# Two halves of a modulation as VectorE's partial sums in the first feed-forward, in place of TensorE's units at the norm changes

## The chip, the cores and the metric

The kernel runs on one core of a Trainium2 chip. Its engines work side by side, each through its own queue in program order, and meet through semaphores: TensorE (PE in the profile; its loads of the stationary operand are PEld), VectorE (DVE), ScalarE (ACT), GpSimd (POOL) and SyncE (SP), which here issues the loads of all weights. The metric is the device time of one launch in microseconds, as the median of several runs.

## The reference, cut to what matters

One step of a diffusion backbone with one layer on 640 tokens of 1024 channels: 128 context tokens and 512 latent ones. Both groups pass the same weights, but each is modulated by a vector of its own. The modulations are one matrix product of a vector with 9216 columns, nine pieces of 1024:

```python
def trunk_layer(x, cond, ...):
    mod = jax.nn.silu(cond) @ w_mod + b_mod
    sh1, sc1, g1, shm, scm, gm, sh2, sc2, g2 = jnp.split(mod, N_MOD, axis=-1)
    h = modulate(rmsnorm(x, norm_g[0]), sh1, sc1)
    x = x + 0.5 * g1[:, None, :] * swiglu(h, ffn1_w1, ffn1_w2)
    h = modulate(rmsnorm(x, norm_g[1]), shm, scm)
    y, C, n, m = mixer(h, ...)
    x = x + gm[:, None, :] * y
    h = modulate(rmsnorm(x, norm_g[2]), sh2, sc2)
    x = x + 0.5 * g2[:, None, :] * swiglu(h, ffn2_w1, ffn2_w2)
```

`swiglu` splits `h @ w1` in two, multiplies `silu(a)` with `b` and applies w2, with 2816 channels inside. Everything is float32. So gm is needed only where the mixer's output joins x, and g2 only where the second feed-forward's output does; shm and scm are needed at the norm before the mixer, sh2 and sc2 at the norm before the second feed-forward.

## The kernel before

The activations lie transposed in SBUF, channels on the partitions. The 640 tokens are two halves of 320 columns (h = 0 is the left half, h = 1 the right). A float32 product is three matmuls on rounded operands (`three`, L245 to L247): each operand is split into a high part, a cast on ACT (L75), and a low part, the difference on VectorE (L79), and high by high, high by low and low by high are summed in PSUM.

**Elements.** The program is a list of elements that `run` goes through in order. Each names its weight loads (raws of 512 KB or less, which go through a ring of five `wr` slots, issued by SP in the order of the elements), the splits of its weights (made four operations ahead of their use) and a function that emits its work. An element can have a `fill`, small steps spread over its products.

- A **pair** (`pair_el`) makes two column blocks of a first product by a scheme of seven half-size products instead of eight. VectorE forms four sums of weights for it (L218). The order is A11, S1, S2, A12, S3, S4, A22, twelve matmuls each. Behind S3, L294 on VectorE adds a saved product to the accumulator that A22 then goes on summing. Behind S4, L297 adds another. The fill's steps are spread over the seven products: four steps land behind the second, fourth, sixth and seventh.
- A **w2 element** (`plain_el`) makes one block of the second product for both halves, and its results are added to the residual x by VectorE (L937), three operations.
- `halves_el` makes the last blocks before a norm change half by half, so that the left half's norm can start while TensorE makes the right half's blocks.
- `head_el` is the first element behind a norm change: three blocks on the left half, then on the right half. Its chain is the norm: the sum of squares (summed at L801, over the partitions by TensorE at L819), the root and reciprocal, the diagonal matrices (L829) and their spread over the partitions on TensorE (L836), scaling (L844), modulation (L852, L854) and the splits into H11, H21 for the left and T4 ("HT4"), H22 for the right half.

The first feed-forward runs through 22 blocks in groups of 6, 6, 6 and 4: pairs, then eight w2 elements for each group (the last group has two and a `halves_el`). Two norm changes follow in the kernel: first feed-forward to mixer, at some 455 to 500 us of the span, and mixer to second feed-forward, at some 1190 to 1230 us.

**Modulations** are made in three ways.

- `mod_mid(ch, half)`: four loads of a quarter, each followed by four matmuls of the vector with 256 columns on four 32-column groups of TensorE (`mod_half`, L574; a float32 matmul leaves two records). `head_el` takes two of the loads before its products and two between the left and the right half. Then come a copy out of PSUM (L581, one on VectorE, one on ACT), four transposes (L586) and a sum and a bias on VectorE (L591, L593), some later. GM's lower half is made so in the mixer's head, and G2's in the second feed-forward's head.
- `mod_dve(ch, halves, wide, joint)`: four loads of 128 x 1024, each with four VectorE operations of 128x512: the first of a sum multiplies (L694), the others multiply and add (L696) into two accumulators, one for each group of tokens. When a half is summed, three steps follow: TensorE sums the partitions with ones on its four column groups and ACT copies (`red`, L705 and L708), two transposes (`turn`, L713), the bias on VectorE (`fin`, L721). With `joint` the three steps of two halves are put together: one `red` step with eight matmuls (16 records), one `turn`, one `fin`.
- `mod_own`: for the first feed-forward's own gate.

`with_units(main, units, spare)` puts the units (a load and its four VectorE operations) into the elements of `main`: the load comes behind the element's own raws, the operations into its fill, and of the three later steps one goes into each following element. With n elements less the spare ones and m units, unit e goes to element floor(e n / m). In the first feed-forward `main` has 42 elements with 2 spare: w2 elements 0 to 7, pairs 8 to 13, w2 14 to 21, pairs 22 to 27, w2 28 to 35, pairs 36 to 39, w2 40 and 41. The accumulators are four tiles of the pool `ma`.

Of the kernel before, what the change touches and what calls it, by code (L numbers as in the profile page):

```python
# [44 lines left out]
def mixer_step(ctx: ExitStack, tc: tile.TileContext, x_prompt, x_sample, state_C, state_n, state_m,  # L45
# [290 lines left out]
    def head_el(blocks, chain, work, mid=(), extra=None):  # L336


        pre, nb = len(mid) // 2, len(blocks)
        order = [None] * pre + [0, 1, 2] + [None] * (len(mid) - pre) + list(range(3, nb))  # L340
        points = 4 * nb - 6
        at_ = {t: i for i, t in enumerate(order) if t is not None}

        def emit():
            flush()
            n = {"i": 0}

            def take(u, i):
                u["emit"](raw(el["base"] + i))
                rdone.add(el["base"] + i)  # L350
                load_more()

            def some(*_):
                n["i"] += 1
                if n["i"] == 3 and soon:
                    soon.pop(0)()
                while len(work) > 0 and n["i"] * total >= points * (total - len(work) + 1):
                    work.pop(0)()

            total = len(work)  # L360
            ev = lambda t: lambda h_, ps: blocks[t][1](h_, ps)
            hold()
            for i in range(pre):
                take(mid[i], i)
            w = [[op()] for t in range(3)]
            ps = [big() for t in range(3)]
            for k in range(KT):
                if k == 4:
                    for t in range(3):
                        w[t].append(op())  # L370
                for t in range(3):
                    three(ps[t][:, :HT], *w[t][k // 4], k % 4, plain_acts(k, 0), k == 0, k == KT - 1)
                if k == 1:
                    chain[0]()
                    for f in N.pop("rest"):
                        f()
                if k == 3:
                    chain[1]()
            for t in range(3):
                ev(t)(0, ps[t][:, :HT])  # L380
            chain[2]()
            for i in range(pre, len(mid)):
                take(mid[i], 3 + i)
            chain[3]()
            for t in range(3):
                unit(w[t], KT, plain_acts, 1, ev(t), {3: some, 7: some})
                release(2)
            if extra:
                extra()
            for t in range(3, nb):  # L390
                w = [op(), op()]
                unit(w, KT, plain_acts, 0, ev(t), {3: some, 7: some})
                unit(w, KT, plain_acts, 1, ev(t), {3: some, 7: some})
            while work:
                work.pop(0)()
            for f in chain[4:]:
                f()
        loads = [b[0] for b in blocks]
        loads = [u["raws"][0] for u in mid[:pre]] + loads[:3] + [u["raws"][0] for u in mid[pre:]] + loads[3:]
        oa = [dict(tile_ops(KT, at_[t])[i], raws=[at_[t]]) for i in range(2) for t in range(3)]  # L400
        ob = [dict(o, raws=[at_[t]]) for t in range(3, nb) for o in tile_ops(KT, at_[t])]
        el = dict(element(loads, oa + ob, emit), calm=True)
        return el

    def blocks_of(p):
        return [(p[i], lambda h, ps, i=i: p[2](i, h, ps)) for i in range(2)]
# [269 lines left out]
    def mod_dve(ch, halves, wide, joint=False):  # L676


        units, posts = [], []
        for half in halves:  # L680
            hold_ = {}
            for kq in range(4):
                fns = []
                for i in range(2):
                    for k in range(2):
                        def fn(w, i=i, k=k, kq=kq, hold_=hold_):
                            if kq == 0 and k == 0:
                                hold_[i] = wide()
                            s = cm[:, 2 * kq + k, i:i + 1]
                            for j, acc in enumerate(hold_[i]):  # L690
                                n = 512 // len(hold_[i])
                                w_ = w[:, 512 * k + j * n:512 * k + j * n + n]
                                if kq == 0 and k == 0:
                                    V.tensor_scalar(acc, w_, s, None, op0=OP.mult)  # L694
                                else:
                                    V.scalar_tensor_tensor(acc, w_, s, acc, op0=OP.mult, op1=OP.add)  # L696
                        fns.append(fn)

                def red(hold_=hold_):

                    p = aux()
                    n = 512 // len(hold_[0])
                    for q in range(4):
                        i, a = q // 2, 256 * (q % 2)
                        PE.matmul(p[32 * q:32 * q + 32, :256], ones[:, :32], hold_[i][a // n][:, a % n:a % n + 256],  # L705
                                  start=True, stop=True, skip_group_check=True, tile_position=(0, 32 * q))
                    hold_["r"] = t3()
                    A.copy(hold_["r"][:, :256], p[:, :256])  # L708

                def turn(hold_=hold_):  # L710
                    p = hold_["p"] = aux()
                    for j in range(2):
                        PE.transpose(p[:, j * P:j * P + P], hold_["r"][:, j * P:j * P + P], ident)  # L713

                def fin(ch=ch, half=half, hold_=hold_):
                    b0 = ch * KT + 4 * half
                    o = modT[:, ch, 4 * half:4 * half + 4, :].rearrange("p (c j) i -> p i c j", c=2)
                    src = hold_["p"][:, :256].rearrange("p (j i c r) -> p i c j r", j=2, i=2, c=2)[:, :, :, :, 0]
                    b = bmT[:, b0:b0 + 4].rearrange("p (c j) -> p c j", c=2)
                    for i in range(2):  # L720
                        V.tensor_add(o[:, i], src[:, i], b)  # L721
                if kq == 3:
                    posts.append((red, turn, fin))
                more = []
                if kq == 3 and (not joint or half == halves[-1]):
                    more = [lambda fs=fs: [f() for f in fs] for fs in zip(*posts)]
                    posts = []
                units.append((mod_load(ch, half, kq), fns, more))
        return units

    def with_units(main, units, spare=0):

        out = []
        n, m = len(main) - spare, len(units)
        e = 0
        post = []
        for i, el in enumerate(main):
            el = dict(el, raws=list(el["raws"]), fill=list(el.get("fill", ())))
            now, post = post[:1], post[1:]
            while e < m and e * n < (i + 1) * m:  # L740
                load, fns, more = units[e]
                at_ = len(el["raws"])
                el["raws"].append(load)
                for j, fn in enumerate(fns):
                    def go(fn=fn, at_=at_, el=el, last=(j == len(fns) - 1)):
                        fn(raw(el["base"] + at_))
                        if last:
                            rdone.add(el["base"] + at_)
                            load_more()
                    el["fill"].append(step(go))  # L750
                post += [step(f) for f in more]
                e += 1
            el["fill"] += now
            out.append(el)
        assert e == m
        return out + [step(lambda: lazy.extend(p["emit"] for p in post))]
# [534 lines left out]
    main = []  # L1291
    for i in range(3):
        main += els[i][1] + els[i + 1][0]
    w2s = els[3][1]
    prog += with_units(main + w2s[:-1], mod_dve(SHM, (0, 1), ma_wide, True) + mod_dve(SCM, (0, 1), ma_wide, True) +
                   mod_dve(SH2, (0,), ma_wide), 2)
    prog += [step(gain(1, SCM)), step(lambda: PO["ma_x"].close()), w2s[-1]]


# [450 lines left out]

    h0 = head_q(0)
    chain, work = right_chain(1, SHM)
    prog.append(head_el(blocks_of(h0[0]) + blocks_of(h0[1]), chain, work, mod_mid(GM, 0), gate_rows))
    def tanh_first():
        A.activation(tp.tile([P, 3], F32, name="rstd", bufs=2)[:, 0:1], eps, AF.Tanh)

# [230 lines left out]
            YQ.append(y_out)  # L1987

    PO["y"] = y_queue
    head, els = ffn(ffn2_w1, ffn2_w2, G2, y_after, lambda bl: head_el(bl, *right_chain(2, SH2), mod_mid(G2, 0)))  # L1990
    prog += [head] + els[0][0] + [step(half_gate(G2))]
    for i in range(3):
        prog += els[i][1] + els[i + 1][0]
# [30 lines left out]
```

## Time and profile before

| | |
|---|---|
| median of 3 runs | 1662.88 us (1662.47 to 1663.27) |
| span of the profiled execution | 1659.7 us (the page gives no time of its own beside it) |
| granted TensorE clock, mean | 0.999 |
| TensorE busy | 1642.4 us |
| VectorE busy | 1257.6 us |
| ACT busy | 791.5 us |

A line of the timeline reads: start and length in us, engine, line of the kernel, operation, output <- inputs, shape, count, and in brackets how long the engine had been idle before it and who ended the wait. Two matmuls of a stream overlap in the records: 0.31 us is the length of one, but the next one starts about 0.15 us behind it. So what an insertion costs TensorE is read from the starts around it. A line of the page's groups gives line, engine, operation, operands, count | busy us, mean ns of one | idle before it. A line of the chain gives start, us, engine, output and line.

### The profile page before, as it was taken

To read this page: it belongs to the slowest core of one execution; us is meant where nothing else is said; L and a number is where in the kernel's file an instruction comes from. 1 tells how busy PE (TensorE), PEld (TensorE's weight loads), DVE (VectorE), ACT (ScalarE), POOL (GpSimd) and SP (SyncE) were. 2 spreads that over 40 slices of the span, in tenths; PEclk is the share of its full clock that TensorE was granted. 3 is DMA by queue.
4 is the path that set the end of the run, shared out by engine and by line. 5 is a ranking of instruction groups with operands and counts; after the bars stand their busy time and mean duration, and the time that the engine had idled before them with its cause. 6 is when DMAs were issued, how large, how long until landed. Compare 5 with 4: busy or idle time off the path is not lost.

```text
span 1659.7 us, 29315 instructions
## 1 busy us (share of the span) xinstructions
PE 1642.4 (99%) x11201; PEld 1601.4 (96%) x11201; DVE 1257.6 (76%) x2681; ACT 791.5 (48%) x1723; POOL 170.7 (10%) x258
## 2 busy tenths in 40 slices
PE   8999999999999999999999999999999999999998
PEld 5999999999999999999999999999999999999997
DVE  6867877877778878778897898789587467476576
ACT  5642542533566656555561455532375245254253
POOL 2010000000031322111121221011100000000002
PEclk9999999999999999999999999999999999999999
DMA  9454333343352434342367323366241322232222
GB/s 321 115 165 127 111 111 111 102 136 101 108 178 80 113 88 111 75 109 67 96 208 239 106 79 92 101 196 207 90 127 55 99 77 79 74 93 87 77 77 64
DMA packets 273036, 193.08 MB, mean 116 GB/s; under 512 B 7923, under 2 KB 253050, under 8 KB 272896
## 3 DMA queue, kind: packets, MB, share of 16 engines
q1 hardware_dynamic: 263280, 158.36, 32.5%
q0 software_dynamic: 9584, 32.85, 6.8%
q8 instruction: 88, 1.44, 0.4%
q14 instruction: 52, 0.43, 0.1%
q10 hardware_dynamic: 32, 0.01, 0.0%
HBM read 175.87 MB, written 15.31 MB: 115 GB/s over the span
## 4 chain that ended last, share of the span: by engine, by line
PE 91%; DVE 3%; ACT 3%; DMA 2%; issue 1%; SPq 1%; POOL 0%; ACTq 0%; DVEq 0%; POOLq 0%
PE ps L245 28%; PE ps L246 28%; PE ps L247 28%; PE ax L1583 2%; PE ax L1614 2%; DMA wr<-in_ffn_w_dram 1%; PE ax L1586 1%; PE ax L1560 1%; ACT Uh L852 1%; DVE wl L79 0%; ACT wh L75 0%; SPq L552 0%; DVE x L937 0%; DMA wl<-in_x_sample_dram 0%; DVE Uh L844 0%
## 5 line engine op out<-in xcount | busy, mean ns | idle before, releaser
L79 DVE TENSOR_TENSOR wl<-wr,wh 128x512 fp32r<-128x512 f32 (+1 forms) x406 | 265.3, 667 | 79.8 <-ACT wh L75 76.5
L75 ACT CAST wh<-wr 128x512 fp32r<-128x512 f32 (+1 forms) x408 | 237.4, 593 | 158.7 <-PE ps L246 146.1
L79 DVE TENSOR_TENSOR wl<-ws,wh 128x512 fp32r<-128x512 f32 x288 | 203.1, 705 | 44.5 <-ACT wh L75 43.8
L75 ACT CAST wh<-ws 128x512 fp32r<-128x512 f32 x288 | 175.7, 619 | 101.2 <-DVE ws L218 60.0
L245 PE MATMUL ps<-Uh,wh 128*128 128x320 f32 x704 | 218.8, 311 | 0.0
L246 PE MATMUL ps<-Ul,wh 128*128 128x320 f32 x704 | 217.2, 309 | 0.0
L247 PE MATMUL ps<-Uh,wl 128*128 128x320 f32 x704 | 217.2, 308 | 0.0
L937 DVE SCALAR_TENSOR_TENSOR x<-ps,modT,x 128x128 f32<-128x128 f32 (+2 forms) x216 | 82.6, 432 | 114.0 <-PE ps L247 114.0
L245 PEld LDWEIGHTS ps<-Uh,wh 128*128 128x128 f32 x704 | 132.1, 188 | 1.2 <-issue 0.8
L246 PEld LDWEIGHTS ps<-Ul,wh 128*128 128x128 f32 x704 | 132.1, 188 | 0.2 <-DVE Ul L79 0.2
L247 PEld LDWEIGHTS ps<-Uh,wl 128*128 128x128 f32 x704 | 132.1, 188 | 0.0
L245 PE MATMUL ps<-H11h,wh 128*128 128x320 f32 x380 | 120.0, 316 | 0.5 <-ACT H11h L75 0.5
L245 PE MATMUL ps<-HT4h,wh 128*128 128x320 f32 x380 | 119.8, 315 | 0.0
L245 PE MATMUL ps<-H21h,wh 128*128 128x320 f32 x380 | 118.9, 313 | 0.0
L246 PE MATMUL ps<-H11l,wh 128*128 128x320 f32 x380 | 117.7, 310 | 0.3
L246 PE MATMUL ps<-HT4l,wh 128*128 128x320 f32 x380 | 117.5, 309 | 0.1
L247 PE MATMUL ps<-H21h,wl 128*128 128x320 f32 x380 | 117.5, 309 | 0.0
L247 PE MATMUL ps<-HT4h,wl 128*128 128x320 f32 x380 | 117.4, 309 | 0.0
L247 PE MATMUL ps<-H11h,wl 128*128 128x320 f32 x380 | 117.4, 309 | 0.0
L246 PE MATMUL ps<-H21l,wh 128*128 128x320 f32 x380 | 117.2, 308 | 0.0
L245 PE MATMUL ps<-H22h,wh 128*128 128x320 f32 x348 | 108.9, 313 | 0.0
L246 PE MATMUL ps<-H22l,wh 128*128 128x320 f32 x348 | 107.7, 309 | 0.4
(440 smaller groups left out, 4475.6 us busy)
## 6 DMA issues: line engine op xcount, KB each, us to landing
wr<-in_ffn_w_dram SPq DMA_DIRECT2D x86, 512.0 KB, 3.8
wr<-in_w_in_dram SPq DMA_DIRECT2D x72, 512.0 KB, 3.7
wr<-in_w_mod_dram SPq DMA_DIRECT2D x51, 512.0 KB, 3.8
wr<-in_ffn_w_dram SPq DMA_DIRECT2D x48, 384.0 KB, 3.4
early<-in_w_mod_dram SPq DMA_DIRECT2D x13, 512.0 KB, 8.4
wr<-in_ffn_w_dram SPq DMA_DIRECT2D x20, 256.0 KB, 3.2
mg<-in_w_mod_dram POOLq DMA_DIRECT2D x8, 512.0 KB, 5.5
wr<-in_w_ml_out_dram SPq DMA_DIRECT2D x8, 512.0 KB, 4.6
```

The source lines that it names most:

```text
L75: A.copy(hi, raw)
L79: V.tensor_sub(lo, raw, f32(hi))
L245: PE.matmul(ps, hi[:, ws], ah, start=start, stop=False, skip_group_check=True)
L246: PE.matmul(ps, hi[:, ws], al, start=False, stop=False, skip_group_check=True)
L247: PE.matmul(ps, lo[:, ws], ah, start=False, stop=stop, skip_group_check=True)
L852: A.activation(t[:, a:b], t[:, a:b], AF.Identity, scale=sc_, bias=bi_)
L937: V.scalar_tensor_tensor(X[m][:, o + a:o + b], ps[:, a:b], modT[:, g, m, cd:cd + 1], X[m][:, o + a:o + b], op0=OP.mult, op1=OP.add)
L1560: PE.matmul(p[:, :P], S["k", dt][:, sl], S["q", dt][:, sl], start=(dt == 0), stop=(dt == 1))
L1583: PE.matmul(p2[:, :DH + 1], S["q", dt][:, sl], S["C"][d][:, dt, :], start=(dt == 0), stop=(dt == 1))
L1586: PE.matmul(p1[:, :DH + 1], S["p", ch][:, d, :], PO["vt"][:, ch, :], start=True, stop=True)
L1614: PE.matmul(p[:, :DH + 1], kw[:, dt * P:(dt + 1) * P], PO["vt"][:, ch, :], start=True, stop=True)
```

## The change

Two lists change. The first feed-forward's units become seven halves in place of five: the lower halves of GM and G2 join SHM, SCM and SH2's lower half, and the three later steps of SHM and SCM are no longer put together. At the heads of the mixer and of the second feed-forward `mod_mid` is taken out.

```diff
-    prog += with_units(main + w2s[:-1], mod_dve(SHM, (0, 1), ma_wide, True) + mod_dve(SCM, (0, 1), ma_wide, True) +
-                   mod_dve(SH2, (0,), ma_wide), 2)
+    prog += with_units(main + w2s[:-1], mod_dve(SHM, (0, 1), ma_wide) + mod_dve(SCM, (0, 1), ma_wide) +
+                   mod_dve(GM, (0,), ma_wide) + mod_dve(SH2, (0,), ma_wide) + mod_dve(G2, (0,), ma_wide), 2)
...
-    prog.append(head_el(blocks_of(h0[0]) + blocks_of(h0[1]), chain, work, mod_mid(GM, 0), gate_rows))
+    prog.append(head_el(blocks_of(h0[0]) + blocks_of(h0[1]), chain, work, (), gate_rows))
...
-    head, els = ffn(ffn2_w1, ffn2_w2, G2, y_after, lambda bl: head_el(bl, *right_chain(2, SH2), mod_mid(G2, 0)))
+    head, els = ffn(ffn2_w1, ffn2_w2, G2, y_after, lambda bl: head_el(bl, *right_chain(2, SH2)))
```

So m goes from 20 to 28 in the first feed-forward. The same weights are loaded, by as many loads of the same size: eight of them move from the heads to the first feed-forward. The upper halves of GM and G2, and G2's factor of one half, stay where they were.

## The prediction

> **What bounds the kernel now.** I read the page first, then busy time by windows, then TensorE's own order of time around the two norm changes, and last VectorE's order inside the first feed-forward, where the change puts its work.
>
> ```profile
> span 1659.7 us, 29315 instructions
> ...
> PE 1642.4 (99%) x11201; PEld 1601.4 (96%) x11201; DVE 1257.6 (76%) x2681; ACT 791.5 (48%) x1723; POOL 170.7 (10%) x258
> ...
> PE 91%; DVE 3%; ACT 3%; DMA 2%; issue 1%; SPq 1%; POOL 0%; ACTq 0%; DVEq 0%; POOLq 0%
> ```
>
> TensorE is busy 99% of the span, and 91% of the chain that ended last is TensorE. So an edit is priced by the time it takes or frees in TensorE's stream, except where TensorE stands waiting for another engine. The next rows (length, then busy time and count of PE, PEld, DVE, ACT, POOL, then granted clock and DMA) show both kinds of stage.
>
> ```profile
> 197.06:209.38 12.32, 12.32 (x86) 12.32 (x85) 10.68 (x20) 6.63 (x14) 0.00 (x0) 1.00 0.46 129
> 450.00:500.00 50.00, 49.15 (x349) 46.17 (x348) 37.99 (x93) 31.81 (x70) 13.24 (x18) 1.00 0.56 172
> ```
>
> The first window is one period of a w1 pair in the first feed-forward: TensorE is full for all 12.32 us, VectorE is busy 10.68 us of it. The second holds the change from the first feed-forward to the mixer: TensorE is short by 0.85 us there, so something else ends last.
>
> **The change part by part.** First the prices. One STT (the accumulating operation of a partial sum) and the matmuls that go:
>
> ```profile
> L696 DVE SCALAR_TENSOR_TENSOR ma<-wr,cm,ma 128x512 f32<-128x512 f32 x70 | 51.6, 747 | 0.9
> ...
> L574 PE MATMUL ax<-wr,cm 128*32 128x256 f32 x64 | 4.3, 385 | 0.0
> ```
>
> A half of a modulation is four loads of 512 KB and 16 VectorE operations; at 0.747 us each that is at most 12.0 us (the two that open the sums are tensor_scalar and no dearer, I take them at the same price). Two halves more (GM's and G2's lower ones) put 23.9 us on VectorE, and eight loads more on SP's queue, between the elements of the first feed-forward. The 64 matmuls of L574 are what goes: 32 at each norm change, in two blocks of 16 records each. What a block costs TensorE is read where nothing waits, at the second norm change:
>
> ```profile
> 1207.59 0.31 PE L247 MATMUL ps<-HT4h,wl 128*128 128x320 f32 x1
> 1207.83 1.07 PE L574 MATMUL ax<-wr,cm 128*32 128x256 f32 x16
> ...
> 1209.08 0.31 PE L246 MATMUL ps<-H11l,wh 128*128 128x320 f32 x1
> ```
>
> From the last matmul before to the second one behind it 1.49 us pass, where two steps of the stream would be 0.29 (0.146 us each: the twelve from 207.41 to 209.16, in the last rows of this part, take 1.75): **1.20 us** a block, 4.80 for the four. The reductions of a partial sum over the partitions (L705) are read alike, for two halves at once (16 records) and for one (8):
>
> ```profile
> 245.95 0.31 PE L247 MATMUL ps<-Uh,wl 128*128 128x320 f32 x1
> 246.19 1.07 PE L705 MATMUL ax<-ma,ones 128*32 128x256 f32 x16
> ...
> 247.44 0.30 PE L246 MATMUL ps<-Ul,wh 128*128 128x320 f32 x1
> ...
> 446.46 0.31 PE L247 MATMUL ps<-HT4h,wl 128*128 128x320 f32 x1
> 446.70 0.64 PE L705 MATMUL ax<-ma,ones 128*32 128x256 f32 x8
> ...
> 447.52 0.31 PE L246 MATMUL ps<-Ul,wh 128*128 128x320 f32 x1
> ```
>
> 1.49 less 0.29 is 1.20 us for a joint block; 1.06 less 0.29 is **0.77 us** for a single one. Two single ones cost 0.34 more than a joint one. The chain prices the transposes behind them:
>
> ```profile
> 252.73 0.44 PE ax L713 x4
> ...
> 451.05 0.22 PE ax L713 x2
> ```
>
> 0.44 us for four and 0.22 for two, so splitting these costs nothing. mod_mid ends in four such transposes as well (0.44).
>
> A rule bears on this: the Trainium skill, "TensorEngine Tiling (Array Packing)", section "Tiling Modes", says that going from one tiling mode of the array to another drains TensorE. It speaks against the change, which replaces two joint reductions by four: without such a cost a block of 8 would be half of one of 16, 0.60 us, the added TensorE work 2 x (0.60 + 0.22) = 1.64 instead of the 2.66 us below, and the sum 1.0 lower. The rows above have that cost in them, so the trace agrees, and they are used.
>
> So in the **first feed-forward** TensorE gets 2 x 0.34 for the joint reductions of SHM and SCM that are split, and 2 x (0.77 + 0.22) for the new halves: **+2.66 us**. Nothing there hides it, as TensorE never waits. Behind the norm changes the transposes of mod_mid go: 2 x 0.44 = **-0.88 us**, in pairs where TensorE is full. ACT's and VectorE's copies, sums and biases move with them, a few tenths beside TensorE's work.
>
> What are the four blocks worth **at the norm changes**? First change, first block:
>
> ```profile
> 478.36 0.48 DVE L79 TENSOR_TENSOR H11l<-Ul,H11h 128x320 fp32r<-128x320 f32 x1
> ...
> 481.62 0.49 DVE L801 TENSOR_TENSOR sqacc<-sqacc,t 128x320 f32<-128x320 f32 x1 [0.67 <-ACT t L797]
> ...
> 478.89 0.41 PE L246 MATMUL ps<-H11l,wh 128*128 128x320 f32 x1
> ...
> 482.17 0.83 PE L819 MATMUL ax<-ones,sqacc 128*128 128x2 f32 x6 [0.52 <-DVE sqacc L801]
> ```
>
> Right behind the block TensorE waits for H11l (VectorE ends it at 478.84, the matmul starts at 478.89), and at 482.17 for the sum of squares, which VectorE ends at 482.11. VectorE's queue there holds the norm's scaling, splits and residual sums, nothing of mod_mid. Without the block TensorE arrives 1.2 us earlier and waits that much longer: 0 gained. The second block comes before the right half's units:
>
> ```profile
> 494.85 0.49 DVE L79 TENSOR_TENSOR H22l<-Uh,H22h 128x320 fp32r<-128x320 f32 x1
> 495.90 0.49 DVE L79 TENSOR_TENSOR H22l<-Ul,H22h 128x320 fp32r<-128x320 f32 x1 [0.56 <-ACT H22h L75]
> ...
> 495.39 0.42 PE L246 MATMUL ps<-H22l,wh 128*128 128x320 f32 x1
> ...
> 496.45 0.41 PE L246 MATMUL ps<-H22l,wh 128*128 128x320 f32 x1
> ```
>
> The matmuls at 495.39 and 496.45 start right when VectorE ends the H22l that they read (495.34, 496.39). Again the block only fills a wait: 0. At the second change:
>
> ```profile
> 1210.58 0.49 DVE L801 TENSOR_TENSOR sqacc<-sqacc,t 128x320 f32<-128x320 f32 x1 [0.61 <-ACT t L797]
> ...
> 1213.98 0.68 DVE L829 TENSOR_SCALAR dg<-ident,rstd 128x128 f32<-128x128 f32 x3
> ...
> 1211.57 0.72 PE L819 MATMUL ax<-ones,sqacc 128*128 128x2 f32 x6
> ...
> 1214.88 0.83 PE L836 MATMUL ax<-dg,ones 128*128 128x128 f32 x6
> ```
>
> Here the sum of squares was there at 1211.07 and TensorE came at 1211.57, so the first block's removal gains at most 0.50 up to there. But the next meeting point, the spread of the row scales at 1214.88, needs three diagonals, which VectorE ends at 1214.66: at most **0.2 us** is left. For the second block there is this:
>
> ```profile
> 1224.48 0.49 DVE L79 TENSOR_TENSOR H22l<-Ul,H22h 128x320 fp32r<-128x320 f32 x1 [0.56 <-ACT H22h L75]
> ...
> 1225.02 0.41 PE L246 MATMUL ps<-H22l,wh 128*128 128x320 f32 x1
> ```
>
> The matmul at 1225.02 waited for H22l (ready at 1224.97), a chain of ACT and VectorE work in which no step of TensorE's left half ends last. Gained: 0. I take -0.1 for the four blocks; the ends are 0 and -4.80.
>
> **VectorE's room** decides the rest. with_units puts unit e on element floor(40 e / m): with m = 20 every second element has one, with m = 28 runs of three neighbours occur. Of the pairs (elements 8 to 13, 22 to 27, 36 to 39) the neighbours 10 and 11, 11 and 12, 24 and 25, 37 and 38 then both hold a unit; before, no two neighbours did. A unit's four operations are issued behind a pair's second, fourth, sixth and seventh product. So from one L297 to the next VectorE has two of them now, and four after the change in these four places. In order of time, with two:
>
> ```profile
> 198.84 0.75 DVE L696 SCALAR_TENSOR_TENSOR ma<-wr,cm,ma 128x512 f32<-128x512 f32 x1
> 199.50 0.69 DVE L218 TENSOR_TENSOR ws<-wr 128x512 f32<-128x512 f32 x1
> ...
> 206.82 0.69 DVE L79 TENSOR_TENSOR wl<-ws,wh 128x512 fp32r<-128x512 f32 x1
> 207.60 0.49 DVE L294 TENSOR_TENSOR t<-ps,t 128x320 f32<-128x320 f32 x1
> ...
> 209.36 0.49 DVE L297 TENSOR_TENSOR t<-ps,t 128x320 f32<-128x320 f32 x1 [0.67 <-PE ps L247]
> ...
> 207.41 0.31 PE L245 MATMUL ps<-H22h,wh 128*128 128x320 f32 x1
> ...
> 209.16 0.31 PE L245 MATMUL ps<-HT4h,wh 128*128 128x320 f32 x1
> ```
>
> From 198.84 on VectorE has no gap but 0.09 us before L294 (206.82 + 0.69 to 207.60). An STT takes 0.66 us of such a stretch (198.84 to 199.50). Two more move L294 by 1.32 - 0.09 = 1.23 us, to end at 209.32. L294 reads the accumulator that the pair's last product goes on summing, and that product starts at 209.16: TensorE waits some 0.2 us. L297's wait of 0.67 then takes back half of the lag. At 11 and 12 a reduction of 0.77 us of TensorE time falls between, and gives VectorE that room; at 24 the two additions of a finished half come on top. I take 0.2 + 0 + 0.4 + 0.2 = **+0.8 us**. Bounds: 0, if the order leaves some slack that I don't see; 4 x 1.32 = 5.3, if all of it is waited for.
>
> A rule stands behind this as well: the Trainium skill, "TensorE: Matmul & The Clock Gate", section "Architectural detail: the array is 16× 32×32, not 1× 128×128", calls ACT's and VectorE's queues strictly first in, first out. By it L294 can't pass the added operations; if it could, the +0.8 would be 0. The rows above stand in the program's order, which agrees.
>
> For the w2 elements of this feed-forward (36 matmuls, 5.3 us) one row is enough, the residual sums of one that holds a unit:
>
> ```profile
> 135.06 1.14 DVE L937 SCALAR_TENSOR_TENSOR x<-ps,modT,x 128x128 f32<-128x128 f32 x3 [0.32 <-PE ps L247]
> ```
>
> Even there VectorE has 0.32 us left and waits for TensorE, so neighbours with units don't add up: 0. The splits of weights run four products (7 us) ahead of their use, so a lag of one or two us doesn't reach them: 0. The added loads take ring slots: a slot is given back when the unit's last operation has run, and the next pair's loads come behind it. In the pairs TensorE has no wait in the row above, and I take 0; a late load would be of the size of the lag, and is in the upper bound. At the norm changes four loads fewer stand ahead of w_in's and the second w1's; these are not waited for: 0.
>
> **Sum:** +2.66 - 0.88 - 0.1 + 0.8 = **+2.5 us** (0.15%). The span is 1659.7 us; the page gives no time of its own for this execution, and the median of the three runs lies 3.2 us above the span, the start and end around it. These don't change, so 1662.9 + 2.5 = **1665.4 us**.
>
> **The rivals.**
> 1. The blocks' time counts: the norm chains move up with TensorE, by a wait that the rows hide. Then -4.80 replaces -0.1: 1660.7; half of it gives 1663. For it speaks that TensorE is full right up to the first block and the second change shows no wait but one. Against it, the waits that stand behind three of the four blocks, and the diagonals behind the fourth. Chance 0.15.
> 2. **VectorE becomes the bound in pairs**: the slower side. From one L297 to the next it then has 12.32 - 0.67 + 1.32 = 12.97 us of work and of waits that it can't fill, against TensorE's 12.32. It decides once L294 ends later than the start of the last product, a lag of 1.07 us. If the lag isn't taken back, each of the four places costs 0.65 us or more, 2.6 together: +2.66 - 0.88 - 0.1 + 2.6 = +4.3, 1667.2. For it: the single gap of 0.09. Against: the reduction between 11 and 12, and 0.67 of slack per pair that has no such neighbours. Chance 0.27.
> 3. No lag at all, or one that L294 never shows: +1.7, 1664.6. Chance 0.2, within the forecast's own range of 1664.3 to 1666.1 (together 0.55).
> The remaining 0.03 is for a transfer that comes late.
>
> **How the numbers follow.** 0.2%, or 3.3 us, is about what a measurement of this kernel can tell from no change: 1659.6 and 1666.2. Faster than that needs all of rival 1 and no lag: 0.05. Slower: rival 2, most of its 0.27, and the late transfer: 0.27. Within: 0.68. The range runs from 1661.0, most of rival 1, to 1668.0, rival 2 with its lag carried on; what lies outside is rival 1 in full and the bound of 5.3, under 2 in 10.
>
> **What would show it.** Right: in the changed profile L574 on wr has only the records of the first norm, L705 has no block of 16 in the first feed-forward but seven of 8, and TensorE's waits at the norm changes for H11l, sqacc and H22l have grown by about 1.2 us a block at the first change; the first feed-forward is 2.7 to 3.5 us longer, and the stages behind them gain 0.4 us each. For the lag: PE waits for L294 in four pairs, 0.2 to 0.4 us each. Wrong: the norm changes are shorter by over 1 us (rival 1), or TensorE waits in pairs sum to over 2 us (rival 2), or VectorE's L294 shows no lag beside doubled units.

## The result

| | median | runs | of the kernel before |
|---|---|---|---|
| before | 1662.78 us | 20 (1661.72 to 1664.11) | |
| changed | 1665.66 us | 20 (1664.35 to 1668.16) | 1.0019, 95% interval 1.0012 to 1.0025 |

The change costs 2.9 us; 2.5 were forecast (1665.4). It is inside the 0.2% that the prediction called about no change, and the interval leaves out 1. Of the runs below, one execution of e2 and one of e6 took several times as long as the others (9190.50 and 4167.74 us) and are not among the runs compared.

The page of the changed kernel, first the span, then the engines, then the chain that ended last by engine:

```profile
span 1663.8 us, 29232 instructions
...
PE 1642.5 (99%) x11149; PEld 1599.3 (96%) x11149; DVE 1277.8 (77%) x2711; ACT 790.9 (48%) x1723; POOL 171.0 (10%) x258
...
PE 91%; DVE 4%; ACT 3%; DMA 1%; issue 1%; SPq 0%; ACTq 0%; DVEq 0%
```

VectorE has 20.2 us more work (1257.6 before). TensorE has 52 records fewer and is as busy to 0.1 us (1642.4 before), in a span that is 4.1 us longer. By the prediction's prices 5.7 us of its work went and 2.7 came, so its busy column holds more than work; the windows below say where. TensorE's groups by line show the edit itself:

```profile
L705 PE MATMUL ax<-ma,ones 128*32 128x256 f32 x56 | 4.5, 391 | 0.0
...
L574 PE MATMUL ax<-wr,cm 128*32 128x512 f32 x12 | 2.1, 605 | 0.0
```

The 64 records of L574 with 256 columns are gone, L705 has 16 more.

A span alone doesn't say where the time went, since two executions already differ ahead of the first changed instruction. So the same six instructions are looked up in both timelines of TensorE (start, length): the first w2 matmul of the first feed-forward, the first statistics at the first norm change, the gate rows at its end, the transposes of L1379 behind the first pair, the first statistics at the second norm change, the first w2 matmul of the second feed-forward. Before:

```profile
119.03 0.31 PE L245 MATMUL ps<-Uh,wh 128*128 128x320 f32 x1
...
467.22 0.83 PE L819 MATMUL ax<-ones,sqacc 128*128 128x2 f32 x6
...
504.41 0.46 PE L1370 MATMUL ax<-Ul,gw 128*32 128x320 f32 x1
...
521.34 0.71 PE L1379 MATMUL ax<-ident,sqacc 128*128 128x128 f32 x5
...
1197.49 0.83 PE L819 MATMUL ax<-ones,sqacc 128*128 128x2 f32 x6 [0.15 <-DVE sqacc L801]
...
1291.44 0.31 PE L245 MATMUL ps<-Uh,wh 128*128 128x320 f32 x1
```

and changed:

```profile
119.92 0.31 PE L245 MATMUL ps<-Uh,wh 128*128 128x320 f32 x1
...
471.79 0.83 PE L819 MATMUL ax<-ones,sqacc 128*128 128x2 f32 x6
...
509.00 0.46 PE L1370 MATMUL ax<-Ul,gw 128*32 128x320 f32 x1
...
525.48 0.71 PE L1379 MATMUL ax<-ident,sqacc 128*128 128x128 f32 x5
...
1201.99 0.83 PE L819 MATMUL ax<-ones,sqacc 128*128 128x2 f32 x6 [0.16 <-DVE sqacc L801]
...
1295.45 0.31 PE L245 MATMUL ps<-Uh,wh 128*128 128x320 f32 x1
```

The differences between neighbours are the lengths of five stages. The changed kernel is 0.89 us late at the first of these rows, ahead of the change. From there: first feed-forward 348.19 to 351.87, **+3.68**; first norm change 37.19 to 37.21, **+0.02**; first pair behind it 16.93 to 16.48, **-0.45**; mixer 676.15 to 676.51, +0.36; second norm change and the pairs behind it 93.95 to 93.46, **-0.49**. The sum is +3.12 us, beside 2.88 by the medians.

Why the norm changes give nothing is in busy time by windows, laid from the first statistics to the end of the right halves (length, then PE, PEld, DVE, ACT, POOL busy with counts, clock, DMA). Before:

```profile
467.22:504.41 37.19, 36.45 (x260) 33.55 (x260) 30.84 (x72) 28.38 (x66) 8.82 (x13) 1.00 0.60 185
1197.49:1225.02 27.53, 27.47 (x207) 25.65 (x207) 22.22 (x55) 23.18 (x52) 2.53 (x2) 1.00 0.41 119
```

Changed:

```profile
471.79:509.00 37.21, 34.70 (x229) 32.73 (x229) 31.67 (x73) 28.39 (x65) 8.81 (x13) 1.00 0.41 128
1201.99:1229.54 27.55, 26.56 (x175) 24.95 (x175) 22.23 (x55) 23.17 (x52) 2.53 (x2) 1.00 0.21 59
```

31 and 32 TensorE records fewer, ACT's work the same, and both stages as long to 0.02 us. VectorE's 0.83 us more in the first stage lie at its end, where it runs ahead into the next pair. TensorE's busy column fell by 1.75 and 0.91 us, less than the 2.40 us that two blocks take, which says that some of the time that counts as busy is waiting (e6 below shows it). The waits that took the blocks' place at the first change stand in the changed kernel's TensorE, and VectorE's split that ends there is where it was:

```profile
483.48 0.41 PE L246 MATMUL ps<-H11l,wh 128*128 128x320 f32 x1 [1.13 <-DVE H11l L79]
...
498.55 0.41 PE L245 MATMUL ps<-H22h,wh 128*128 128x320 f32 x1 [0.52 <-ACT H22h L75]
```

```profile
500.49 0.49 DVE L79 TENSOR_TENSOR H22l<-Ul,H22h 128x320 fp32r<-128x320 f32 x1 [0.56 <-ACT H22h L75]
```

That split starts 28.70 us behind the stage's first row; in the kernel before it started 28.68 us behind (495.90, in the prediction).

### The profile page after: what moved, and what is told of

It is laid out like the page before. It is cut to its first block, busy times and chain, and to the rows that moved or that the text cites. A ratio compares the mean times of both kernels' runs of the same rounds, so it can differ in the third digit from the quotient of the medians.

```text
span 1663.8 us, 29232 instructions
## 1 busy us (share of the span) xinstructions
PE 1642.5 (99%) x11149; PEld 1599.3 (96%) x11149; DVE 1277.8 (77%) x2711; ACT 790.9 (48%) x1723; POOL 171.0 (10%) x258
## 4 chain that ended last, share of the span: by engine, by line
PE 91%; DVE 4%; ACT 3%; DMA 1%; issue 1%; SPq 0%; ACTq 0%; DVEq 0%
PE ps L245 28%; PE ps L246 28%; PE ps L247 27%; PE ax L1583 2%; PE ax L1614 2%; PE ax L1586 1%; DMA wr<-in_ffn_w_dram 1%; DVE wl L79 1%; ACT Uh L852 1%; PE ax L1560 1%; DVE x L937 1%; DVE ma L696 0%; PE ax L705 0%; DVE Uh L844 0%; ACT wh L75 0%
## 5 line engine op out<-in xcount | busy, mean ns | idle before, releaser
L937 DVE SCALAR_TENSOR_TENSOR x<-ps,modT,x 128x128 f32<-128x128 f32 (+2 forms) x216 | 82.7, 433 | 100.1 <-PE ps L247 100.0
```

Source lines behind the costliest of these rows:

```text
L937: V.scalar_tensor_tensor(X[m][:, o + a:o + b], ps[:, a:b], modT[:, g, m, cd:cd + 1], X[m][:, o + a:o + b], op0=OP.mult, op1=OP.add)
```

## The experiments

The theory: TensorE's time in the first feed-forward counts (+2.66), VectorE's sums make it wait there now and then (+0.95 in the changed trace, by the two rows below), the blocks at the norm changes are free, their transposes are not (-0.88). Rivals: the blocks count; the waits have another cause; VectorE is late all along.

The two waits, each with VectorE's rows and then TensorE's. The first is in pair 38, behind pair 37; both hold sums:

```profile
433.39 0.69 DVE L218 TENSOR_TENSOR ws<-wr 128x512 f32<-128x512 f32 x1 [0.41 <-DMA wr<-in_ffn_w_dram]
...
434.61 0.75 DVE L696 SCALAR_TENSOR_TENSOR ma<-wr,cm,ma 128x512 f32<-128x512 f32 x1
...
436.48 0.48 DVE L294 TENSOR_TENSOR t<-ps,t 128x320 f32<-128x320 f32 x1
```

```profile
436.27 0.31 PE L247 MATMUL ps<-H22h,wl 128*128 128x320 f32 x1
437.01 0.42 PE L245 MATMUL ps<-HT4h,wh 128*128 128x320 f32 x1 [0.43 <-DVE t L294]
```

0.74 us from start to start where a step is 0.146: 0.59 us lost. The second is in the first pair behind w2 elements 20 and 21, both with sums:

```profile
280.16 2.98 DVE L696 SCALAR_TENSOR_TENSOR ma<-wr,cm,ma 128x512 f32<-128x512 f32 x4
283.06 1.13 DVE L937 SCALAR_TENSOR_TENSOR x<-ps,modT,x 128x128 f32<-128x128 f32 x3
```

```profile
283.36 0.31 PE L247 MATMUL ps<-H11h,wl 128*128 128x320 f32 x1
283.87 0.39 PE L245 MATMUL ps<-HT1h,wh 128*128 128x320 f32 x1 [0.20 <-DVE x L937]
```

0.51 less 0.146 is 0.36 us lost: the residual sums L937, which give an accumulator back, stand behind four sums in a row. No other wait of TensorE stands in this feed-forward, and none at all before.

The change and the eight runs by the same six instructions. The first five columns are the change of each stage against the kernel before in us, the sixth their sum, the last the difference of the medians with the interval of the ratio:

| run | first FF | first change | first pair | mixer | second change | sum | medians |
|---|---|---|---|---|---|---|---|
| changed | +3.68 | +0.02 | -0.45 | +0.36 | -0.49 | +3.12 | +2.88 (1.0012 to 1.0025) |
| e1_split_alone | +0.58 | 0.00 | 0.00 | +0.01 | -0.04 | +0.55 | +0.54 (0.9991 to 1.0009) |
| e2_mid_out | +0.01 | +0.29 | -0.45 | +0.26 | -0.48 | -0.37 | +0.27 (0.9991 to 1.0009) |
| e3_units_and_mid | +3.60 | +0.02 | 0.00 | +0.01 | -0.06 | +3.57 | +3.57 (1.0009 to 1.0027) |
| e4_no_sums | +3.00 | 0.00 | -0.45 | +2.04 | -0.40 | +4.19 | +4.06 (1.0014 to 1.0032) |
| e5_spread | +2.61 | 0.00 | -0.45 | +0.02 | -0.41 | +1.77 | +1.42 (1.0002 to 1.0020) |
| e6_mid_twice | +0.01 | +0.01 | 0.00 | 0.00 | +1.41 | +1.43 | +1.32 (0.9998 to 1.0017) |
| e7_late_red | +2.16 | 0.00 | -0.01 | +0.37 | -0.41 | +2.11 | +1.36 (0.9999 to 1.0017) |
| e8_all | +0.24 | 0.00 | 0.00 | +0.07 | -0.49 | -0.18 | -0.29 (0.9989 to 1.0007) |

The medians tell most of these runs from each other only just. The stages tell more, but each is from one profiled execution, and stages that an edit doesn't touch moved by up to 0.37 us (2.04 in e4). The two columns agree within 0.8 us.

**e1: the split alone**, in the kernel before:

```diff
-    mod_dve(SHM, (0, 1), ma_wide, True) + mod_dve(SCM, (0, 1), ma_wide, True) +
+    mod_dve(SHM, (0, 1), ma_wide) + mod_dve(SCM, (0, 1), ma_wide) +
```

> The kernel before with one thing changed: the two halves of SHM, and those of SCM, are reduced one by one, four blocks of 8 records (0.77 us) in place of two of 16 (1.20). My theory, that TensorE's own time in the first feed-forward counts in full: 2 x 0.34 = +0.7 us to the kernel before, with no new wait of TensorE in the first feed-forward. A rival, that such a block's fixed part lies in time that TensorE loses anyway: 0.0. Another, that a reduction of one half waits for VectorE's last sum where the joint one had the second half's time to come: more than +1.5, with a wait ahead of L705 in the trace.

The first feed-forward grew by 0.58 us, every other stage stayed to 0.04, and no wait came: the two joint blocks' saving is real, close to the 0.68 of the rows.

**e2: the blocks out**, in the kernel before, with nothing in their place:

```diff
-    prog.append(head_el(..., mod_mid(GM, 0), gate_rows))
+    prog.append(head_el(..., (), gate_rows))
...
-    head_el(bl, *right_chain(2, SH2), mod_mid(G2, 0))
+    head_el(bl, *right_chain(2, SH2))
...
+        for ch in (GM, G2):
+            G.memset(modT[:, ch, 0:4], 0.1)
```

> The kernel before with the four blocks and the transposes of the lower halves of GM and G2 at the norm changes left out, and nothing in their place: these two halves are not computed, a constant stands for them. My theory, that TensorE waits at the norm changes for VectorE and ScalarE whether it has the blocks or not, so that only the transposes behind them count: 2 x 0.44 = -0.9 us to the kernel before, with TensorE's waits grown by about 2.4 us at each change. A rival, that the blocks' time counts in full: 4.8 + 0.9 = -5.7 us. One between, that they are free at the first change alone: -0.9 - 2.4 = -3.3.

Busy time of e2 in the windows used above:

```profile
469.09:506.57 37.48, 34.70 (x228) 32.72 (x228) 31.93 (x73) 28.39 (x65) 9.06 (x13) 1.00 0.41 127
1199.46:1227.02 27.56, 26.57 (x176) 24.97 (x176) 22.25 (x55) 23.07 (x52) 2.54 (x2) 1.00 0.21 59
```

32 and 31 records of TensorE less, and the stages are 0.29 and 0.03 us longer than before. The transposes gave 0.45 and 0.48 us. Both rivals (-5.7 and -3.3) are far outside the interval, which ends at -1.5 us. The median shows none of the 0.9; by the stages 0.29 went at the first change and 0.26 in the mixer, neither of which I foresaw. The first is one split on VectorE ahead of H11l, here in e2 and then in the changed kernel:

```profile
477.88 1.37 DVE L79 TENSOR_TENSOR wl<-wr,wh 128x512 fp32r<-128x512 f32 x1 [0.25 <-ACT wh L75]
```

```profile
480.58 1.03 DVE L79 TENSOR_TENSOR wl<-wr,wh 128x512 fp32r<-128x512 f32 x1 [0.24 <-ACT wh L75]
```

It took 0.34 us longer, and TensorE waited that much longer for H11l, within 0.05: further evidence that VectorE ends that stretch. GpSimd works on the sum of squares (L801) beside it in both; whether that slowed it was not tested. In the mixer 0.25 us are lost at one place, the transposes at 602.26 (L1572 in e2, L1570 before), and why is open.

**e3: blocks and units both**: the changed kernel with the two calls of mod_mid back.

> The changed kernel with the old units at the norm changes put back beside the new ones: the two lower halves are computed twice. My theory: the blocks cost nothing, their transposes 2 x 0.44, so +0.9 us to the changed kernel and 2.9 + 0.9 = +3.8 to the kernel before. The rival that the blocks' time counts: +5.7 to the changed kernel, +8.6 to the kernel before. If eight loads more in the middle of it bind the queue of transfers, a wait for wr would show at the first norm change.

+3.57 us to the kernel before, where 3.8 were expected and the rival gave 8.6. By the stages it is +3.60 in the first feed-forward and nothing beyond 0.06 behind it. So the whole of the change's gain, with the blocks taken out, is the two rows of -0.45 and -0.49.

**e4: without the new halves' sums**:

```diff
                             for j, acc in enumerate(hold_[i]):
+                                if ch in (GM, G2) and (kq or k):
+                                    continue
```

> The changed kernel with 14 of the 16 VectorE operations of each of the two new halves left out (28 of 0.747 us: 20.9 us of VectorE), loads, reductions and transposes kept: the two halves get wrong sums. My theory, that VectorE's additions cost only the two waits that TensorE shows in the first feed-forward (0.36 us at the first pair behind w2 elements, 0.59 us in a pair that follows a pair): -0.9 us to the changed kernel, +2.0 to the kernel before. The rival that those waits come from TensorE's own new order or from the transfers: 0.0 to the changed kernel, +2.9 to the kernel before. The rival that VectorE ends late all along the pairs: -2 us or more to the changed kernel, +0.9 or less to the kernel before.

The time rose instead, and by the median alone the theory would have fallen. By stages the first feed-forward is 0.68 us shorter than the changed kernel's: the wait for L294 is gone, the one for L937 has stayed. That agrees with sums in neighbours as the cause, since pairs 37 and 38 held sums of G2, which are left out here, and the sums of elements 20 and 21 are of SCM, which are not. The rival that VectorE is late all along (-2 us or more) is out. What hid the gain is in the mixer, 2.04 us longer. For most of that ScalarE waits for a tile that is read back from memory (timeline of ScalarE):

```profile
864.55 1.02 ACT L1809 ACTIVATE Bh<-x,halves 128x320 fp32r<-128x320 f32 x2 [0.58 <-DMA x<-rd]
869.48 1.01 ACT L1809 ACTIVATE Bh<-x,halves 128x320 fp32r<-128x320 f32 x2 [1.09 <-DMA x<-rd]
```

No such wait stands in the kernels before and after. Why this reload lands later in e4 is open; no run was spent on it. The other 0.35 is what the changed kernel has there too (see the end of the next section).

**e5: no neighbouring pairs**: the changed kernel with the same 28 units on listed elements.

```diff
+    PLACE = (0, 1, 2, 3, 4, 5, 6, 8, 10, 12, 14, 15, 16, 18, 19, 20, 22, 24, 26, 28, 29, 30, 31, 32, 33, 34, 36, 38)
...
-            while e < m and e * n < (i + 1) * m:
+            while e < m and (PLACE[e] <= i if m == 28 else e * n < (i + 1) * m):
```

> The changed kernel with the 28 loads of the first feed-forward and their sums set on listed elements, so that no two w1 pairs in succession carry one and none lies on the last w2 element of a stretch. My theory, that the two waits of TensorE there (0.36 us of lost time at the pair behind elements 20 and 21, which both carry sums, and 0.59 in pair 38 behind pair 37) come from VectorE's sums in neighbours: both go, -0.9 us to the changed kernel, +2.0 to the kernel before. A rival, that VectorE is then late in the w2 elements, six or seven of which in succession carry sums: the waits move there and nothing is gained, +2.9 or more. If the 0.36 at the w2 elements' end has nothing to do with neighbours, only 0.6 goes: +2.3.

TensorE has no wait left in the first feed-forward, and the stage is 2.61 us longer than before: the 2.66 us of its own work, to 0.05. Against the changed kernel 1.07 us are gone there. The places of the units (their loads and their sums), not their number, were the cause of both waits. Runs of seven w2 elements with units stand in e5 and made no wait, so what is left as the cause is units in neighbouring pairs and in the element right ahead of a pair. The median fell further (1.42 against 2.0 expected), 0.34 of it in the mixer.

**e6: the blocks twice**, in the kernel before:

```diff
-                for j in range(4):
+                for r, j in [(r, j) for r in range(1 if wide else 2) for j in range(4)]:
...
-    start=(k < 4), stop=(k >= 4),
+    start=(k < 4 and not r), stop=(k >= 4 and bool(r or wide)),
```

> The kernel before with the matmuls of each block at the norm changes issued twice (32 records in place of 16, so the two halves come out doubled): 16 records more are 16 x 0.054 = 0.86 us a block, 3.4 for the four. My theory, that the blocks are free only as long as the chain on VectorE and ScalarE ends later, and that the kernel before has used that up (its TensorE shows only one wait there, 0.67 us of lost time ahead of the statistics at the first change, 0.2 at the second): 3.4 - 0.9 = +2.5 us to the kernel before. A rival, that TensorE's work is free at the norm changes without such an end: 0.0. Another, that nothing hides it at all: +3.4.

Half of it: +1.41 us at the second change, near the 1.52 foreseen (1.72 less 0.2), but 0.01 at the first, where I had counted one wait of 0.67 us as all the room. The rest of the room is in rows that carry no wait. TensorE's timeline of the kernel before, in the right half at the first change:

```profile
494.91 0.38 PE L245 MATMUL ps<-H22h,wh 128*128 128x320 f32 x1
495.39 0.42 PE L246 MATMUL ps<-H22l,wh 128*128 128x320 f32 x1
495.65 0.31 PE L247 MATMUL ps<-H22h,wl 128*128 128x320 f32 x1
495.93 0.41 PE L245 MATMUL ps<-H22h,wh 128*128 128x320 f32 x1
496.45 0.41 PE L246 MATMUL ps<-H22l,wh 128*128 128x320 f32 x1
```

and the same matmuls in e6, 0.96 us later by the clock when they begin (0.07 of it from ahead of the change):

```profile
495.87 0.31 PE L245 MATMUL ps<-H22h,wh 128*128 128x320 f32 x1
496.02 0.31 PE L246 MATMUL ps<-H22l,wh 128*128 128x320 f32 x1
496.17 0.31 PE L247 MATMUL ps<-H22h,wl 128*128 128x320 f32 x1
496.31 0.31 PE L245 MATMUL ps<-H22h,wh 128*128 128x320 f32 x1
496.54 0.41 PE L246 MATMUL ps<-H22l,wh 128*128 128x320 f32 x1
```

Before, starts lie 0.48, 0.26, 0.28 and 0.52 us apart, 1.54 us for four steps that take 0.58 when nothing is missing. In e6 the four take 0.67, and at the last row the two kernels meet again (496.45 and 496.54). So TensorE waited 0.96 us for the H22 tiles before, and no row has it as idle time: it is in the starts and in lengths of 0.4 in place of 0.31.

**e7: reductions in the wait**: the changed kernel, with SH2's and G2's sums kept until the first norm change.

```diff
+    held = mod_dve(SH2, (0,), ma_wide) + mod_dve(G2, (0,), ma_wide)
+    HELD = [u[2] for u in held if u[2]]
+    held = [(u[0], u[1], []) for u in held]
...
+    def red_late(f=chain[3]):
+        f()
+        for h_ in HELD:
+            h_[0]()
+        for j in (1, 2):
+            lazy.append(lambda j=j: [h_[j]() for h_ in HELD])
+
+    chain[3] = red_late
```

(The pool of the sums is closed behind the norm change in place of ahead of it.)

> The changed kernel with the reductions of the lower halves of SH2 and G2 taken out of the first feed-forward and issued behind one another at the first norm change, ahead of the right halves, where TensorE of the changed kernel waits for H22; their transposes follow in the next pair. My theory: -2 x 0.99 us in the first feed-forward, 0 for the 16 records (1.20 us) in the wait, +0.44 for the four transposes: -1.5 to the changed kernel, +1.4 to the kernel before. A rival, that the copies on ScalarE or the block itself hold up the chain that ends there: -0.3 to the changed kernel, +2.6 to the kernel before.

The block of 16 stands in the norm change, and the same wait for H22 behind it:

```profile
494.24 1.07 PE L705 MATMUL ax<-ma,ones 128*32 128x256 f32 x16
...
498.01 0.41 PE L246 MATMUL ps<-H22l,wh 128*128 128x320 f32 x1
```

The stage is 37.19 us, as long as without the block: 1.20 us of TensorE cost nothing there. The four transposes cost their 0.44 (the first pair gives 0.01 in place of 0.45). The first feed-forward gained 1.52 of 1.98. Of the rest, 0.06 is a longer wait for L294 in pair 38 (0.80 us from start to start, 0.74 in the changed kernel) and 0.06 a longer one for the statistics; 0.22 lies in the starts of one w2 element (0.27 and 0.25 apart at 452.56 and 452.83), without idle time in a row, and why is open.

**e8: all of it**: e5's places, e7's late reductions, and SHM and SCM joint again.

> The two runs before this one's parts together (the listed elements, the late reductions of SH2 and G2), and SHM's and SCM's halves again reduced two at a time. My theory, by the sum of the terms: 2.9 - 0.9 - 1.5 - 0.7 = -0.2 us to the kernel before. A rival, that a term is counted twice (the wait ahead of the joint reduction, or the room at the norm change): +1 or more to the kernel before. No theory makes it clearly faster than the kernel before.

-0.18 us by the stages, -0.29 by the medians, with 1 well inside the interval: the terms add up here, and there is no kernel here that beats the one before by what can be measured.

## Why the prediction was right

- **TensorE's own work in the first feed-forward, +2.66**: right. e5, where nothing waits, has +2.61; e1 has 0.58 for the part that was put at 0.68.
- **The four blocks, -0.1 with an end at -4.80**: right, and nearer to 0. Both norm changes are as long without them (+0.02, and 27.53 to 27.55 us). The first rival fell with e2 and e3. What carried this step was the row that showed who ends last (VectorE's H22l, ready 0.05 us ahead of TensorE's step), not the busy shares, which had TensorE full.
- **The transposes, -0.88**: right: -0.45 and -0.49, 0.94 together. e3 keeps them and has 0.00 and -0.06.
- **VectorE's lag, +0.8 in four pairs at 0.2, 0, 0.4 and 0.2**: the size came out near (1.07 by e5), but by luck. Three of the four pairs cost nothing, the fourth cost 0.59, and 0.36 came from w2 elements, which were put at 0. So the prediction's own sign, waits of 0.2 to 0.4 us for L294 in four pairs, was not seen, and the first feed-forward is longer (3.68) than its 2.7 to 3.5. L294 was late, as the prediction said, but a lag has to exceed 1.07 us before TensorE sees it: the prediction's own rows have L294 begin at 207.60, end 0.49 later, and the product that waits for it at 209.16. In the changed kernel L294 and that product stand so at pairs 11 and 25:

```profile
210.41 0.48 DVE L294 TENSOR_TENSOR t<-ps,t 128x320 f32<-128x320 f32 x1
...
329.71 0.49 DVE L294 TENSOR_TENSOR t<-ps,t 128x320 f32<-128x320 f32 x1
```

```profile
211.15 0.31 PE L245 MATMUL ps<-HT4h,wh 128*128 128x320 f32 x1
...
330.68 0.31 PE L245 MATMUL ps<-HT4h,wh 128*128 128x320 f32 x1
```

  It ends 0.26 and 0.48 us ahead of the product: lags of 0.81 and 0.59, both covered, where I had 1.23 (+0.2) and enough for +0.4. Two things were wrong in the step. First, the room ahead of L294 was not the 0.09 us between the end of one record and the start of the next. VectorE's records overlap like TensorE's: a split of 0.69 us is followed by the next start 0.60 us on, and the last two starts ahead of L294, 0.63 and 0.78 apart (206.19, 206.82, 207.60), leave 0.03 + 0.18 = 0.21. Second, not every place gets two full STTs of 0.66 us on top. VectorE's timeline of the changed kernel shows the two that pair 11 gets, and one at pair 24:

```profile
206.34 0.48 DVE L694 TENSOR_SCALAR ma<-wr,cm 128x512 f32<-128x512 f32 x1
206.74 0.69 DVE L79 TENSOR_TENSOR wl<-wr,wh 128x512 fp32r<-128x512 f32 x1
207.34 0.74 DVE L696 SCALAR_TENSOR_TENSOR ma<-wr,cm,ma 128x512 f32<-128x512 f32 x1
...
317.23 0.74 DVE L696 SCALAR_TENSOR_TENSOR ma<-wr,cm,ma 128x512 f32<-128x512 f32 x1
```

  The first opens a half and takes 0.40 us, the second 0.66: 1.06 - 0.21 = 0.85, and 0.81 was measured. The one at 317.23 runs ahead of L297, where VectorE had 0.67 us of waiting to lose, so that only one STT and the two small additions of a finished half (L721, 0.14) come on top in the stretch behind it: 0.66 + 0.14 - 0.21 = 0.59, as measured.

  In pair 38 both are STTs, and a load came late on top: its L218 starts 1.08 us behind the split before it, 0.48 more than a step (0.41 of it stands in its row above as a wait for the load). That makes 1.32 - 0.21 + 0.48 = 1.59, and L294 is 1.66 late (1.07 of margin and 0.59 of wait). SP issued a load at 429.14, right behind the end of the sum that starts at 428.37, having waited 9.7 us for a sum to give a slot back, and VectorE's wait fits that load; no run tested it by itself. This is the "late load of the size of the lag" that the prediction had only in its upper bound.

  And the w2 elements, put at 0, gave 0.36 us where two with four STTs each follow each other ahead of a pair: the row of L937 with 0.32 us of room was of an element whose neighbour held none. Neighbours alone don't do it: elements 34 and 35 hold units too, two of whose operations are the cheaper opening ones, and there L937 ends at 402.64, 0.38 us ahead of the product at 403.02.
- **The second rival, VectorE as the bound**, had the right mechanism for one of its four places (0.59 us against its 0.65), and a lag was never carried on; TensorE's waits in pairs are 0.59 us in all, not 2.6. The third, no lag, is what e5's places give: +1.77 by the stages against its +1.7.
- **Not foreseen:** +0.36 us in the mixer, which no part of the change touches. No wait holds it. The TensorE matmul at 927.12 us before stands 4.14 us later in the changed kernel (931.26), the one at 1092.09 stands 4.49 later (1096.58), and the 0.35 gathers evenly in between, in rows that are full in both kernels at a granted clock of 1.00. The same stretch gives 0.35 in e4 and e7 too, and nothing in the other six runs; why is open. The whole stage gave 0.00 to 0.07 in five of the other runs, 0.26 (at another place) in e2, 0.37 in e7 and 2.04 in e4. The +0.36 cancelled part of the transposes' gain in the stages' sum; that the total came out so near is in part luck.

## What to carry to other kernels

Where another engine ends a stage, work that TensorE does inside its waits is free as long as the waits hold it (e6), and moving it into a stage where TensorE is full turns it into cost: look for the end of the chain first, and move work towards the wait (e7), not out of it. How much a wait still holds is read from the starts of the rows, not from the idle column; that goes for VectorE's room as for TensorE's. Work for an engine that has room on average is best kept out of neighbouring pairs and out of the element right ahead of one; that alone was worth 1.07 us here.

## What the runs showed of the hardware

- A stretch in which TensorE's rows show almost no idle time held 0.96 us of waiting, as starts up to 0.52 us apart in place of 0.146. The Trainium skill, "Perfetto Trace Analysis", section "Tensor Engine Instruction (MATMUL, LD_WEIGHTS)", says that the end of a TensorE record is estimated from the size of the instruction and a delay, not observed. The rows agree: lengths of 0.31 us stand beside starts 0.146 us apart.
- Sixteen records more within a block add 0.87 us (at the second change the H11 matmul stands 1.00 us behind the block's start before, 1207.83 to 1208.83, and 1.87 in e6, 1207.92 to 1209.79): the other 0.33 us of a block's 1.20 is paid once for each block, and e1, with two blocks more, is 0.58 longer. The Trainium skill, "TensorEngine Tiling (Array Packing)", section "Key Properties" under "Tiling Modes", has the array drain at a change of mode; a fixed part for each block agrees with that, and the page gives no figure for it.
- Ahead of the first changed instruction the profiled executions of one and the same code lie up to 1.9 us apart (119.03 us before, 120.89 in e2), more than most of the terms weighed here. Here spans of two profiles are compared from a common instruction on.
